# Hand-made semaphore waits, and quarter-row tiles over the end of a row-maximum kernel

## The chip, the cores and the metric

The kernel runs on one core of one Trainium2 chip. The metric is the device time of one execution in microseconds (us). "Before" measured 1261.12 us as the median of three runs (1261.06 to 1261.18).

## The reference

```python
# x: (32, 2048, 2048) float32, about one element in ten is NaN; axis = -1
def reference(x, axis):
    return np.nanmax(x, axis=axis).astype(np.float32)
```

The input is 536.87 MB and the output is 65,536 numbers, so the kernel is a stream: nearly all of its time is the loading of the input.

## The kernel before

The 65,536 rows stand on 128 partitions, 512 rows of 2048 elements on each. A tile is seven rows a partition (the very first has one). Every tile is described by three lists: its loads, its pieces and its row maxima. Each piece runs through three engines:

1. ScalarE makes a 16-bit key from the upper half of each element, in which a NaN stands for the smallest number.
2. GpSimd, or ScalarE itself where the count is negative (a "back-copy"), writes the cleaned upper halves back into the tile.
3. VectorE takes row maxima of the tile as ordinary floats.

There are three buffers for tiles and three for keys, and a key buffer holds three rows. A load may start when the last maximum of the tile that had its buffer is done.

```python
TILES = (
    [([1], [1], [1])]
    + [ ([7], [2, 3, 2], [2, 3, 2]), ([7], [2, 3, 2], [2, 3, 2]), ([7], [2, 3, -2], [2, 3, 2]) ] * 19
    # ... [cut: fifteen tiles whose loads and pieces get smaller] ...
    + [([1, 1, 1, 1, 1, 1, 1], [1, 1, 1, -1, 1, 1, -1], [1, 1, 2, 1, 1, 1])]
)
GROUPS = [TILES[:14]] + [TILES[i : i + 12] for i in range(14, 74, 12)]
# ... [cut] ...
        for loads, pieces, reds in g:
            xt = io.tile([P, WIDE * D], i32, tag="xt")          # one of 3
            at = 0
            for c in loads:
                nc.sync.dma_start(out=xt[:, at * D : (at + c) * D], in_=xg[...])
                at += c
            # ... [cut]
            for c in pieces:
                back, c = c < 0, abs(c)
                xp = xt[:, at * D : (at + c) * D]
                if used + c > KEYS:                             # a new key buffer
                    kt = mid.tile([P, KEYS * D], u16, tag="kt") # one of 3
                    used = 0
                # ... [cut: ScalarE key, then ScalarE or GpSimd back into xt]
                while reds and done + reds[0] <= at:
                    n = reds.pop(0)
                    nc.vector.tensor_reduce(out=acc[...], in_=xt[...], op=ALU.max)
        # after each group: two small VectorE instructions on its maxima
        # ("the flags", for rows without any number); all stores at the very end
```

A scheduler derives the waits between these instructions from the buffers, and it may also reorder the instructions of one engine.

## Time and profile before

| | before |
|---|---|
| device time, median | 1261.12 us |
| span of the profiled run | 1259.46 us |
| first input packet starts | 1.75 us |
| last input packet ends (called **E** below) | 1245.97 us |
| VectorE's last instruction ends | 1256.50 us, E + 10.53 |
| from there to the span's end | 2.96 us |

How to read it: the time is the start, the transfer, and what follows the last packet. The transfer takes 99% and cannot be shortened by reordering work, so the argument is about a dozen microseconds at the end. The prediction shows the lines for this. It also uses the costs of one row by shape, from the groups split by shape (line, engine, operation and tiles, count; then busy us and mean ns of one; then idle time before them):

```profile
L153 DVE TENSOR_REDUCE acc<-xt 128x1 f32<-128x2048 f32 x20 | 44.6, 2276 | 9.2 <-POOL xt L142 9.2
L125 ACT ACTIVATE kt<-xt,top 128x2048 uint16<-128x2048 int16 x45 | 87.3, 1990 | 6.6 <-DMA xt<-in_x_dram 6.5
L142 POOL TENSOR_SCALAR xt<-kt 128x2048 int16<-128x2048 uint16 x34 | 84.3, 2481 | 14.1 <-ACT kt L125 11.9
L134 ACT ACTIVATE xt<-kt 128x2048 int16<-128x2048 uint16 x11 | 27.4, 2488 | 0.3
```

One row thus costs 1.99 us for a key, 2.48 us for the cleaning on either engine, and 2.28 us for the maximum. One after the other that is 6.75 us.

### The profile page before, as it was taken

What the parts mean: (1) busy time and instruction counts of PE and PEld (TensorE: products, weight loads), DVE (VectorE), ACT (ScalarE), POOL (GpSimd) and SP (SyncE); (2) the same over time, 40 slices, a digit from 0 to 9 for tenths busy, and PEclk for the clock granted to TensorE, in tenths of its full rate; (3) what the DMA queues carried; (4) which work ended last, traced back from release to release, by engine and by line L of the source; (5) the groups of instructions that cost most, each with busy time, mean ns of one, the idle gap of its engine ahead of it and who ended that gap; (6) DMA issues with size and microseconds to landing.
All of it is one profiled execution on the core that took longest, in us unless ns stands there. A gap on an engine that the chain in (4) does not pass through costs nothing.

```text
span 1259.5 us, 1258 instructions
## 1 busy us (share of the span) xinstructions
DVE 1115.2 (89%) x242; ACT 1053.3 (84%) x281; POOL 1091.2 (87%) x219
## 2 busy tenths in 40 slices
DVE  0888898888899898888989888999888889999999
ACT  4788797887888878878888788797887899799997
POOL 2989989889898898898988989889889896999996
DMA  9999999999999999999999999999999999999995
GB/s 412 437 437 437 437 424 421 437 438 437 435 433 435 417 435 437 437 435 435 435 426 424 437 437 434 435 435 436 419 433 437 433 438 435 420 432 429 427 425 214
DMA packets 14697, 537.21 MB, mean 427 GB/s; under 512 B 2400, under 2 KB 2400, under 8 KB 2400
## 3 DMA queue, kind: packets, MB, share of 16 engines
q1 hardware_dynamic: 14688, 537.14, 98.9%
q14 instruction: 9, 0.07, 0.0%
HBM read 536.87 MB, written 0.26 MB: 426 GB/s over the span
## 4 chain that ended last, share of the span: by engine, by line
DMA 29%; POOL 27%; ACT 20%; issue 17%; DVE 7%; SPq 0%; ACTq 0%; POOLq 0%; DVEq 0%
DMA xt<-in_x_dram 29%; POOL xt L142 27%; ACT kt L125 16%; DVE acc L153 7%; ACT xt L134 4%; SPq L110 0%; DVE none L164 0%; DVE acc L173 0%; ACTq L125 0%; POOLq L142 0%; DVEq L153 0%; ACTq L134 0%
## 5 line engine op out<-in xcount | busy, mean ns | idle before, releaser
L153 DVE TENSOR_REDUCE acc<-xt 128x2 f32<-128x4096 f32 (+2 forms) x229 | 1112.6, 4916 | 140.0 <-POOL xt L142 140.0
L142 POOL TENSOR_SCALAR xt<-kt 128x4096 int16<-128x4096 uint16 (+2 forms) x215 | 1091.0, 5074 | 159.1 <-ACT kt L125 146.7
L125 ACT ACTIVATE kt<-xt,top 128x4096 uint16<-128x4096 int16 (+2 forms) x247 | 927.9, 3821 | 196.7 <-DMA xt<-in_x_dram 196.5
L134 ACT ACTIVATE xt<-kt 128x4096 int16<-128x4096 uint16 (+1 forms) x32 | 127.5, 3983 | 1.0
L94 ACT ACT_TABLE_LOAD x1 | 1.3, 1283 | 0.7 <-PEq L193 0.7
L164 DVE TENSOR_SCALAR none<-acc 128x84 int32<-128x84 f32 (+1 forms) x6 | 1.5, 251 | 0.2
L173 DVE TENSOR_TENSOR acc<-acc,none 128x84 int32<-128x84 int32 (+1 forms) x6 | 1.5, 243 | 0.2
L92 DVE MEMSET top<- 128x1 f32 x1 | 0.1, 59 | 0.8 <-PEq L193 0.8
L193 POOL MEMSET const-float32-0.0<- 128x1 f32 x1 | 0.1, 99 | 0.2 <-issue 0.2
L94 ACT ACTIVATE warm<-top 128x1 f32<-128x1 f32 x1 | 0.2, 203 | 0.0
L193 POOL MEMSET const-uint8-127<- 128x1 uint8 x1 | 0.1, 103 | 0.0
L193 POOL MEMSET const-bfloat16-1.0<- 128x1 bf16 x1 | 0.1, 102 | 0.0
L193 POOL MEMSET const-float32-1.0<- 128x1 f32 x1 | 0.1, 99 | 0.0
## 6 DMA issues: line engine op xcount, KB each, us to landing
xt<-in_x_dram SPq DMA_DIRECT2D x63, 7168.0 KB, 23.5
xt<-in_x_dram SPq DMA_DIRECT2D x10, 2048.0 KB, 25.3
xt<-in_x_dram SPq DMA_DIRECT2D x5, 3072.0 KB, 16.1
xt<-in_x_dram SPq DMA_DIRECT2D x13, 1024.0 KB, 23.2
xt<-in_x_dram SPq DMA_DIRECT2D x3, 4096.0 KB, 25.1
xt<-in_x_dram SPq DMA_DIRECT2D x1, 6144.0 KB, 23.3
xt<-in_x_dram SPq DMA_DIRECT2D x1, 5120.0 KB, 18.5
out_dram<-acc SPq DMA_DIRECT2D x5, 42.0 KB, 10.7
```

The lines of the kernel that those rows point to most:

```text
L92: nc.vector.memset(top, EDGE)
L94: nc.scalar.activation(out=warm, in_=top, func=ACT.Prelu, alpha=0.5)
L125: nc.scalar.activation(out=kp, in_=xp.bitcast(i16)[:, 1::2], func=ACT.Prelu, bias=top, scale=-1.0, alpha=float(TOP - LOW) / (EDGE - NAN),)
L134: nc.scalar.activation(out=xp.bitcast(i16)[:, 1::2], in_=kp, func=ACT.Copy, bias=float(TOP), scale=-1.0,)
L142: nc.gpsimd.tensor_scalar(out=xp.bitcast(i16)[:, 1::2], in0=kp, scalar1=-1.0, scalar2=float(TOP), op0=ALU.mult, op1=ALU.add,)
L153: nc.vector.tensor_reduce(out=acc[:, base + done : base + done + n], in_=xt[:, done * D : (done + n) * D] .bitcast(f32) .rearrange("p (c d ...
L164: nc.vector.tensor_scalar(out=none, in0=acc, scalar1=NONE, scalar2=float(0x00C00000), op0=ALU.is_equal, op1=ALU.mult,)
L173: nc.vector.tensor_tensor(out=bits, in0=bits, in1=none, op=ALU.bitwise_or)
L193: nc = _bacc.Bacc("TRN2", target_bir_lowering=False, num_devices=1)
```

## The change

The scheduler's waits are replaced by hand-made ones: a class notes for every instruction which semaphore values it needs, drops those already implied, and puts the last one on the instruction itself. And counts become quarter rows, so that the last eighteen tiles (56 to 73 in the diff) can be cut finer. The last group, twelve tiles before, becomes ten and two, so that the last store has 14 columns, not 84. The maxima stay whole rows everywhere: all their counts are multiples of four. There are 112 loads for 96, 255 pieces for 247 and 226 maxima for 229.

```diff
+Q = D // 4
-    + [([7], [2, 3, 2], [2, 3, 2])] * 2
-    + [([1, 6], [-1, 3, 1, -2], [4, 3])]
... [cut]
-    + [([1, 1, 1, 1, 1, 1, 1], [1, 1, 1, -1, 1, 1, -1], [1, 1, 2, 1, 1, 1])]
+    + [([28], [12, -8, 8], [20, 8])]
+    + [([28], [11, 12, -5], [8, 20])] * 3
... [cut]
+    + [([4, 3, 2, 3, 4, 3, 1, 1, 1, 1, 2, 2, 1], [4, -2, 1, 2, 3, 4, 3, -2, 1, 2, 3, -1], [4, 4, 4, 4, 4, 4, 4])]
-GROUPS = [TILES[:14]] + [TILES[i : i + 12] for i in range(14, 74, 12)]
+GROUPS = [TILES[:14]] + [TILES[i : i + 12] for i in range(14, 62, 12)] + [TILES[62:72], TILES[72:]]
+LANES = 14
+class Order:
... [cut]
+    def add(self, who, engine, issue, deps, lane=None, step=1):
+        want = self.needed(who, deps)
+        for s, v in want[:-1]:
+            engine.wait_ge(self.sems[s], v)
+        inst = issue()
+        for s, v in want[-1:]:
+            inst._wait_ge(self.sems[s], v)
+        name = lane or who
+        inst.then_inc(self.sem(name), step)
... [cut: loads take turns at 14 semaphores, "lanes"; a load waits for the last load of its lane]
+                    if used + c > KEYS:
+                        key = (key + 1) % NKEYS
+                        used = 0
+                        kold, kfree[key] = kfree[key], []
+                        if at + c == sum(loads) * Q:
+
+                            kold = kold + kfree[(key + 1) % NKEYS]
... [cut: the same operations as before, each through add()]
```

When the last piece of a tile opens a new key buffer, its ScalarE instruction waits for that buffer but also for the users of the next one.

## The prediction

> **What bounds the kernel now.** I read the page first (shares, slices, queues), then the groups split by shape, the waits of the engines and of the loading queue, and last the timeline and narrow windows over the end.
>
> ```profile
> span 1259.5 us, 1258 instructions
> DVE 1115.2 (89%) x242; ACT 1053.3 (84%) x281; POOL 1091.2 (87%) x219
> ...
> GB/s 412 437 437 437 437 424 421 437 438 437 435 433 435 417 435 437 437 435 435 435 426 424 437 437 434 435 435 436 419 433 437 433 438 435 420 432 429 427 425 214
> ...
> q1 hardware_dynamic: 14688, 537.14, 98.9%
> q14 instruction: 9, 0.07, 0.0%
> ```
>
> The input is 536.87 MB and the load queue is busy 98.9% of the span. The dips in the GB/s row are packets that straddle a slice's edge: in the packet records loads follow each other without a hole from 1.75 us to the end. So the body is transfer time, and 1259.5 us can shrink only at the two ends.
>
> ```profile
> SPq L110 <- DVE acc L153: 1072.0, 66, 27.0
> SPq L110 <- DVE none L164: 84.6, 5, 17.1
> SPq L110 <- DMA xt<-in_x_dram: 27.7, 8, 9.6
> ```
>
> This is the loading queue's own list. It waits nearly always for the row maxima to free a buffer; the scheduler's waits for an older load cost 27.7 us of the queue's time, but only late in the run. By the records even the tightest load there is issued over 3 us before its first packet starts, and the one-row loads of the last tile some 17 us before. None of these waits empties the transfer engines.
>
> ```profile
> 1095.28 28.30 DVE L153 TENSOR_REDUCE acc<-xt 128x3 f32<-128x6144 f32 x8 [1.60 <-POOL xt L142]
> 1124.93 56.28 DVE L153 TENSOR_REDUCE acc<-xt 128x3 f32<-128x6144 f32 x12 [1.35 <-POOL xt L142]
> 1182.00 73.94 DVE L153 TENSOR_REDUCE acc<-xt 128x4 f32<-128x8192 f32 x22 [0.79 <-POOL xt L142]
> 1255.97 0.25 DVE L164 TENSOR_SCALAR none<-acc 128x84 int32<-128x84 f32 x1
> 1256.26 0.24 DVE L173 TENSOR_TENSOR acc<-acc,none 128x84 int32<-128x84 int32 x1
> ...
> 1243.00:1244.00 1.00, 1.00 (x1) 1.00 (x2) 0.00 (x0) 1.00 0.91 254
> 1244.00:1245.00 1.00, 1.00 (x2) 1.00 (x1) 0.00 (x0) 1.00 0.24 82
> 1245.00:1246.00 1.00, 1.00 (x2) 1.00 (x2) 0.47 (x1) 1.00 0.13 41
> ```
>
> Two things set the end. VectorE runs its last 22 maxima (34 rows, 73.94 us) without a gap, so it is behind when data stops. And data stops raggedly: most transfer engines are done by 1243.4, the slowest at 1245.97 (the DMA share falls 0.91, 0.24, 0.13). From that last packet to the end of the last VectorE instruction (1256.50) are **10.53 us**; store and closing barriers take 2.96 more, and the measured time is 1.66 above the span.
>
> **What the Trainium skill says.** "DMA: Bandwidth & Descriptors", section "Where 436 GB/s comes from", gives a port ceiling of 435 GB/s; the 437 of the full slices agrees, so the body is at the limit. "ScalarE: Activation LUTs", section "What ACT_TABLE_LOAD costs", gives 280 ns + 0.833 ns per element for an ACTIVATE with a pointer bias, and about 93 ns of overlap back to back. The trace agrees: 1990, 3698 and 5402 ns at 2048, 4096 and 6144 elements. "VectorE: DVE Perf Modes", section "The DRAIN you can't avoid", says a semaphore after each operation cost nothing extra in its test; here separate wait records take about 0.02 us and stand beside running work. "Runtime: NRT & Kernel Launch", section "Instruction fetch mechanics", says a sequencer fetches its program by DMA as it runs, sequentially, in 16 KiB blocks. The trace has nine such packets during the run, of 8192 bytes each; each holds one of the 16 transfer engines for about 0.31 us.
>
> **The change, part by part.**
>
> *Waits.* The builds hold 390 separate wait or semaphore instructions before on the four engines (110 ScalarE, 100 VectorE, 99 GpSimd, 81 Sync) and 55 after. At 0.02 us that is under 7 us over four engines, beside work and under the transfer time: worth 0 in the body. Indirectly, the instructions of the four fall from 1259 to 970, so perhaps five fetches instead of nine. The slowest transfer engine is about 2.6 us behind the fastest at the end, of which some 0.35 is there from the first load; if the rest follows the fetches, four fewer give 4/9 of 2.3, about 1.0. I take **-0.8 us** on the last landing.
>
> *Loads.* 112 instead of 96. In the packet records 8192 bytes take 0.312 us and 57,344 take 2.121, so 27.2 bytes per ns and 10.5 ns a packet. An engine moves 8 packets a load: 16 x 8 x 10.5 ns = **+1.35 us**.
>
> *The hand-made section.* Its builds show one more branch and one hop over Sync's semaphore before the first load, and after the last store another hop, a drain on each engine, three semaphore steps and a branch. Closing steps in this trace stand 0.06 to 0.09 us apart: **+0.15 us** at the head, **+0.45 us** at the tail.
>
> *Quarter rows.* The maxima stay whole rows (all counts are multiples of four quarters), so VectorE's work is unchanged, 226 maxima for 229. What shrinks is what lies ahead of them. From the groups by shape, for one, two, three and four quarters: ScalarE key 0.71, 1.14, 1.57, 1.99 us; ScalarE back-copy (2488 and 4766 ns) 0.78 and 1.35 for one and two; GpSimd (2481 and 4772 ns) 0.77, 1.34, 1.91, 2.48; VectorE 2.28 a row, the next starting 2.19 after.
>
> I step through the last tile by hand, with E the last packet and 0.45 us to ScalarE (an estimate from the 0.48 to 0.54 us idles there). Counting the last loads back from E: the ninth lands at E-3.96, the eleventh at E-1.98, the twelfth at E-0.69.
> - Pieces six to eight keep ScalarE busy from E-7.47 to E-2.95, the eighth's back-copy to E-1.57.
> - Piece nine (one quarter) ends at E-0.98, piece ten (two) at E+0.07; GpSimd cleans ten by E+1.49, and row six is whole.
> - Piece eleven (three quarters) waits for ScalarE, not for data: E-0.02 to E+1.55; GpSimd to E+3.54.
> - Piece twelve (one quarter): E+1.46 to E+2.17, back-copy to E+2.98.
> - VectorE: row six E+1.53 to E+3.81, row seven E+3.72 to E+6.00; the two flag instructions end at **E+6.56**.
>
> Against 10.53 before this saves 3.97 us, if VectorE reaches the last tile without arrears. It gets the chance: in the old timeline its gaps from 1020 us on add to 10.4 us, each for a first piece not yet clean, and the new tiles there begin with smaller pieces. The same hand chain with the old one-row pieces gives about E+7.85, so VectorE's arrears were 2.7 us of the 10.53.
>
> *Sum.* Last landing 1245.97 + 1.35 + 0.15 - 0.8 = 1246.67; VectorE's end 1253.23; with 2.96 + 0.45 the span is 1256.64; with 1.66 the time is **1258.3 us**, 2.8 less than now.
>
> **The rivals.**
> - *Arrears stay.* If VectorE is still 2.7 us behind, the end is about 1261.0. For: it runs at 2.19 us a row against 2.42 that a row takes to arrive (16.94 us by the records for seven), so it catches up only 0.23 a row. Against: the 10.4 us of gaps. Perhaps one in five, mostly in part.
> - *The loading queue starves.* Three new tiles end with a five-row maximum, 10.8 us (an estimate from the row of shapes, 2.14 a row and 0.14) where two rows took 4.41, so their buffers come free up to 6.4 us later. Loads lead by some 3 to 5 us there; the tiles' shorter last pieces give part of it back, and I reckon 0.5 to 1.3 us of lead left. A hole would add itself to the end, at most about 1 us a tile, and less where the slowest transfer engine still has work. It would make 1259 to 1261.
> - *Waits were the cost.* If the removed waits bound the body, the time would fall by more than 5 us. The 98.9% and the gapless loads speak against it: transfers alone reach to about 1244, and a whole row's maximum and the store must follow. More than 2% (25 us) would need transfers above the port ceiling.
> - *Small loads are dearer.* Packets of 2048 bytes are not in the old trace; were they twice as dear as the line gives, the five one-quarter loads would cost 3 us more. Unlikely, since 8192 bytes lie on the line.
>
> **Range and chances.** 1258.3 in the middle; fewer fetches or a cheaper section give 1256.3 at best, arrears or a starved tile 1260.8. Nothing here approaches 25 us: same 0.98, faster 0.01, slower 0.01.
>
> **What would show it.** Right: VectorE's last instruction ends 6 to 7.5 us after the last packet (10.53 now), its last idle lies after 1235 us rather than at 1182, no hole between loads, fewer instruction packets on q14, about 3.4 us from there to the span's end. Wrong: a gapless VectorE from before 1200 to the end (arrears), a falling DMA share near 1000 to 1040 us (starving), or a first packet well after 1.9 us (the section's entry). A DMA share far below 1 in the body, or a gain above 6 us, would overturn the whole reading.

## The result

| | before | after |
|---|---|---|
| device time, median of 4 runs | 1261.09 us (1260.92 to 1261.18) | 1258.3 us (1257.99 to 1258.64) |
| ratio, 95% interval | | 0.9978 (0.9961 to 0.9995) |
| span of the profiled run | 1259.46 us | 1256.86 us |
| first input packet | 1.75 us | 1.97 us |
| last input packet, E | 1245.97 us | 1247.23 us |
| VectorE's end | E + 10.53 | E + 6.76 |
| from there to the span's end | 2.96 us | 2.87 us |

The change gains 2.8 us or 0.2%. The span's 2.60 us are 1.26 us lost at E, 3.77 gained after it and 0.09 gained in the tail.

The page of the kernel after, in the lines that answer to those shown of before (busy time, GB/s in 40 slices, and the queues with packets, MB and share of 16 engines):

```profile
span 1256.9 us, 966 instructions
DVE 1115.5 (89%) x241; ACT 1058.2 (84%) x292; POOL 1093.9 (87%) x224
...
GB/s 413 438 436 429 420 438 438 438 433 429 423 438 438 436 436 433 418 438 438 436 436 433 420 436 438 438 436 431 418 438 436 434 409 432 432 430 428 426 422 277
...
q1 hardware_dynamic: 17136, 537.14, 99.3%
q14 instruction: 8, 0.07, 0.0%
```

VectorE works as long as before, and the counted instructions fall from 1258 to 966 without a change in the GB/s of the full slices. The loading queue stays as it was: its own list of waits (us in total, times, longest) has the maxima as the reason, and the scheduler's waits for older loads are no longer there.

```profile
SPq L206 <- DVE acc L174: 1068.7, 65, 36.8
SPq L206 <- DVE none L174: 84.9, 5, 17.3
```

The end of the timeline (start, length, engine, line and operation, how many, idle time before and what ended it), and two narrow windows (length, then busy shares of VectorE, ScalarE and GpSimd with instructions, then clock, DMA share and GB/s):

```profile
1222.45 22.08 DVE L174 TENSOR_REDUCE acc<-xt 128x1 f32<-128x2048 f32 x10
1244.71 8.86 DVE L174 TENSOR_REDUCE acc<-xt 128x1 f32<-128x2048 f32 x4 [0.17 <-POOL xt L170]
1253.82 0.17 DVE L174 TENSOR_TENSOR acc<-acc,none 128x14 int32<-128x14 int32 x1
...
1246.00:1247.00 1.00, 1.00 (x2) 1.00 (x3) 0.92 (x2) 1.00 0.93 234
1247.00:1248.00 1.00, 1.00 (x1) 1.00 (x2) 0.81 (x2) 1.00 0.22 46
```

VectorE now waits for data once more, at 1244.71, where before it had run without a gap since 1182.00. After that last wait it has four rows left. At 1245.97 the old kernel's data was complete; here input packets still keep about 3 of the 16 transfer engines busy between 1246 and 1247 us, so the end is won although data arrives later. The DMA share of 0.93 in that window is not the input: by the packet sizes about four fifths of it are the stores of the earlier groups, which were issued behind the loads and start only as engines finish theirs. Of the 0.91 between 1243 and 1244 us, which the prediction reads as the end of the data, about two thirds are stores too.

One thing in the engines' waits I had not predicted. It is ScalarE's list after:

```profile
ACT kt L166 <- DMA xt<-in_x_dram: 141.3, 52, 15.0
ACT kt L166 <- POOL xt L170: 48.3, 37, 2.6
```

Before, ScalarE waited for loads only, 196.5 us in 49 times. Now it waits for GpSimd 37 times, 48.3 us in all. This is the early key wait.

### The profile page after: what moved, and what is told of

Same layout as the page of the kernel before. It is cut to its first block, busy times and chain, and to the rows that moved or that the text cites. A ratio compares the mean times of both kernels' runs of the same rounds, so it can differ in the third digit from the quotient of the medians. Undisturbed runs are those within 1.5% of the kernel's fastest.

```text
span 1256.9 us, 966 instructions
## 1 busy us (share of the span) xinstructions
DVE 1115.5 (89%) x241; ACT 1058.2 (84%) x292; POOL 1093.9 (87%) x224
## 4 chain that ended last, share of the span: by engine, by line
POOL 51%; ACT 29%; DVE 10%; DMA 8%; issue 1%; SPq 1%; ACTq 0%; DVEq 0%
POOL xt L170 51%; ACT kt L166 22%; DVE acc L174 10%; DMA xt<-in_x_dram 8%; ACT xt L166 7%; SPq L206 1%; DVE none L174 0%; ACTq L105 0%; SPq L355 0%; DVEq L105 0%; SPq L105 0%; SPq L162 0%
## 5 line engine op out<-in xcount | busy, mean ns | idle before, releaser
L174 DVE TENSOR_REDUCE acc<-xt 128x2 f32<-128x4096 f32 (+3 forms) x226 | 1112.7, 4980 | 137.0 <-POOL xt L170 136.8
L170 POOL TENSOR_SCALAR xt<-kt 128x4096 int16<-128x4096 uint16 (+9 forms) x220 | 1093.7, 4971 | 156.9 <-ACT kt L166 143.8
L166 ACT ACTIVATE kt<-xt,top 128x4096 uint16<-128x4096 int16 (+10 forms) x255 | 934.7, 3712 | 190.3 <-DMA xt<-in_x_dram 141.3
L166 ACT ACTIVATE xt<-kt 128x4096 int16<-128x4096 uint16 (+6 forms) x35 | 125.8, 3596 | 1.1
```

What stands on the lines that cost most here:

```text
L166: return order.add("act", nc.scalar, lambda: nc.scalar.activation(**kw), deps)
L170: "pool", nc.gpsimd, lambda: nc.gpsimd.tensor_scalar(**kw), deps
L174: return order.add("dve", nc.vector, lambda: do(**kw), deps)
```

## The experiments

**My theory** after the result: the waits themselves are worth nothing, and the gain comes from the new tiles: VectorE's arrears taken away in the middle ones, and a shorter last chain in tile 73. **The rivals:** the hand-made waits bring the gain; the loading queue is starved near 1020 us and some gain is lost there; the last store or the number of load semaphores matters. The first four kernels below ran together, beside before at 1261.28 us; the other eight ran later in two sets of four, with a median of 1261.34 us for before in either. Each time is the median of five runs. All results were correct.

### Hand-made waits with the old tiles

```diff
-TILES = ( ... quarter-row tiles ... )
+TILES = [tuple([n * 4 for n in counts] for counts in tile) for tile in ROW_TILES]   # tiles of before
-GROUPS = ... [TILES[62:72], TILES[72:]]
+GROUPS = [TILES[:14]] + [TILES[i : i + 12] for i in range(14, 74, 12)]
```

> The hand-made order of waits with the old tiles (every count times four) and the old groups. Theory A (the gain is the finer work at the end; waits are worth nothing in the body, and only shorten the last landing by fewer instruction packets): VectorE is as much in arrears as before, so 1260.6 us, at most 0.8 below the old kernel, with 6 to 8 instruction packets on q14 instead of 9 and the slowest transfer engine some 1.8 us behind the fastest instead of 2.6. Theory B (the waits gave the gain): 1258.3 us, as the whole change.

Measured: 1268.93 us (1268.84 to 1269.05), ratio 1.0061 (1.0048 to 1.0073). This is 7.65 us *slower* than before, and neither theory had it. ScalarE's waits and the timeline show where it goes:

```profile
ACT kt L166 <- POOL xt L170: 69.0, 39, 5.5
...
1084.27 15.21 DVE L174 TENSOR_REDUCE acc<-xt 128x3 f32<-128x6144 f32 x3 [3.09 <-POOL xt L170]
1089.09 14.51 ACT L166 ACTIVATE kt<-xt,top 128x6144 uint16<-128x6144 int16 x4 [4.79 <-POOL xt L170]
1101.68 28.31 DVE L174 TENSOR_REDUCE acc<-xt 128x3 f32<-128x6144 f32 x8 [2.20 <-POOL xt L170]
1109.06 14.88 ACT L166 ACTIVATE kt<-xt,top 128x4096 uint16<-128x4096 int16 x6 [5.46 <-POOL xt L170]
```

The early key wait stops ScalarE for 4.79 and 5.46 us, VectorE goes without work for 3.09 and 2.20 us, its buffers come free late, and the loads run dry: the GB/s row of this run falls to 397 and 413 in two of the slices from 1077 us, where before has 420 and 432. E moves from 1245.97 to 1249.90 us. So I had overlooked a part of the change: a wait *added*.

### The new tiles under the old scheduler

```diff
 # before.py, with Q = D // 4 and every count in quarters:
-TILES = ( ... ); GROUPS = ... range(14, 74, 12)
+TILES = ( ... of after ... ); GROUPS = ... [TILES[62:72], TILES[72:]]
```

> The new tiles and groups under the old scheduler's waits. Theory A: 1258.5 to 1259.2 us, nearly the whole gain; some 0.2 us earlier first load, but nine or more instruction packets and a slowest transfer engine 2.6 us behind. Theory B: 1261 us or more. A third possibility: the scheduler's eight load semaphores hold back the one-quarter loads, and the transfer engines run empty in the last tile; then over 1260 and a DMA share well below 1 before 1244 us.

Measured: 1259.20 us (1259.08 to 1259.40), ratio 0.9984 (0.9971 to 0.9996). The tiles alone give 2.1 of the 2.8 us. The rest is seen in the timelines round tile 56, first of this kernel, then of the change:

```profile
968.44 4.74 ACT L144 ACTIVATE xt<-kt 128x4096 int16<-128x4096 uint16 x1
973.27 19.47 DVE L163 TENSOR_REDUCE acc<-xt 128x5 f32<-128x10240 f32 x3 [6.94 <-issue]
```

```profile
964.54 4.76 ACT L166 ACTIVATE xt<-kt 128x4096 int16<-128x4096 uint16 x1
969.44 19.53 DVE L174 TENSOR_REDUCE acc<-xt 128x5 f32<-128x10240 f32 x3 [1.17 <-POOL xt L170]
```

The scheduler puts ScalarE's third key ahead of the second piece's back-copy, so the back-copy starts at 968.44 and not at 964.54 us, and the five-row maximum that needs it starts 3.8 us later. The tile's buffer comes free at 988.4 instead of 984.6, the next load is issued at 988.48, and the packet records show overlong packets there and a hole: for 0.19 us no engine has an input packet, and from 987.4 us until the new load starts each engine stands idle for 1.7 us on average. The hand-made waits keep the order of the program. That, rather than any cheaper wait, is what I find the hand-made part to be worth here; it fits the difference of about 0.9 us between the medians (of different rounds) and of 0.65 us between the two Es (1247.88 and 1247.23), but I did not test it by giving the scheduler the other order.

### Only the last tile new

```diff
 # tiles of before, but
+TILES[73] = ([4,3,2,3,4,3,1,1,1,1,2,2,1], [4,-2,1,2,3,4,3,-2,1,2,3,-1], [4]*7)
```

> Hand-made waits, the new last tile, the old tiles before it. If VectorE's arrears set the old end (theory A), the finer last tile alone is worth little: about 1260.4 us, VectorE without a gap from about 1182 us on. If the last tile's own chain from landing to maximum set it (theory C), most of the gain shows: about 1258.5.

Measured: 1269.19 us (1268.99 to 1269.31), ratio 1.0062. The early key wait hid whatever this was to show; its repeat without that wait stands below.

### Only the middle tiles new

```diff
-TILES[73] = ([4,3,2,3,4,3,1,1,1,1,2,2,1], [4,-2,1,2,3,4,3,-2,1,2,3,-1], [4]*7)
+TILES[73] = ([4]*7, [4,4,4,-4,4,4,-4], [4,4,8,4,4,4])      # the old one-row tile
```

> Hand-made waits, the new tiles before the last, the old one-row last tile. Theory A (both ends are needed: arrears worked off, and a short last chain): about 1260.2 us, VectorE with an idle gap after 1230 us because it has caught up, last instruction 8 to 9 us after the last packet. If arrears alone were the cause: about 1258.5.

Measured: 1261.07 us (1260.89 to 1261.67), ratio 0.9999 (0.9985 to 1.0012). VectorE has caught up, and it does not help:

```profile
1244.66 5.76 ACT L168 ACTIVATE kt<-xt,top 128x2048 uint16<-128x2048 int16 x3
1244.82 6.70 DVE L176 TENSOR_REDUCE acc<-xt 128x2 f32<-128x4096 f32 x2 [2.17 <-ACT xt L168]
1250.45 2.48 ACT L168 ACTIVATE xt<-kt 128x2048 int16<-128x2048 uint16 x1
1251.78 4.48 DVE L176 TENSOR_REDUCE acc<-xt 128x1 f32<-128x2048 f32 x2 [0.27 <-POOL xt L172]
1256.51 0.17 DVE L176 TENSOR_TENSOR acc<-acc,none 128x14 int32<-128x14 int32 x1
```

It idles 2.17 us before the last rows and ends at E + 9.54 all the same (E is 1247.13 here). The one-row keys queue at ScalarE: three run back to back from 1244.66, and only then follows the last row's back-copy. So without arrears the old last tile still takes 9.54 us after the last packet, of the 10.53 before. The early key wait plays no part in this: from 1180 us on ScalarE waits for loads alone here. Theory A fits in kind, with 9.54 us for the 8 to 9 expected and a time 0.9 us above its figure.

### No early key wait, old tiles

```diff
-                        if at + c == sum(loads) * Q:
-
-                            kold = kold + kfree[(key + 1) % NKEYS]
```

> The hand-made waits with the old tiles, without the three lines that let the last key piece of a tile also wait for the next key buffer (each buffer is still waited for by its own next user). The first waits-only kernel took 1268.9 us, and ScalarE waited 69.0 us for GpSimd there, which the old kernel never does. If that early wait is the cause (theory D), the ScalarE waits for GpSimd fall to near 0 and the time to 1260.6, within 0.6. If the hand-made waits are slow in another way, it stays above 1265.

Measured: 1261.52 us (1261.41 to 1261.77), ratio 1.0002 (0.9989 to 1.0014).

```profile
ACT kt L166 <- DMA xt<-in_x_dram: 196.6, 48, 14.9
...
1182.29 73.95 DVE L174 TENSOR_REDUCE acc<-xt 128x4 f32<-128x8192 f32 x22 [0.76 <-POOL xt L170]
```

ScalarE no longer waits for GpSimd at all, and the 7.4 us are back. VectorE's last stretch is the one of before, 73.95 us for 22 maxima, 0.3 us later. The time is 0.3 us above the range that was expected, and not below before: removing the scheduler's waits is worth nothing, within 0.14% either way. E came 0.24 us earlier here (1245.73) and that did not help, because VectorE is in arrears.

### No early key wait, with the change's tiles

The same three lines are taken out of the kernel after.

> The changed kernel without the early wait for the next key buffer. Theory D: ScalarE's 48.3 us of waits for GpSimd go, the loads of the body are issued about 1 us earlier ahead of their first packets (2.2 to 2.7 us now, 3.6 to 3.9 in the old kernel), and the long first packets from 885 to 1000 us go. The end gains little, since the tiles at the end were cut for that wait: 1257.6 to 1258.4 us. If the early wait earns something by saving wait instructions, the time would rise.

Measured: 1258.48 us (1257.97 to 1258.52), ratio 0.9976 (0.9962 to 0.999). The early key wait costs nothing that can be told with the new tiles, and it earns nothing, though it saves instructions: without it the trace has 1032 and with it 966. From 1040 us on ScalarE waits for GpSimd for about 1.0 us in all, against 15.1 us with the old tiles (and without the early wait it waits 1.0 us there for itself): the new pieces seldom open a key buffer where the next one is still in use. As expected, the overlong packets from 885 to 1000 us are gone; those from 1004 us on stay. The time is just above the range expected.

### No early key wait, only the last tile new

The same three lines are taken out of the kernel of "only the last tile new".

> As the earlier kernel with only the last tile new (1269.2 us), but without the early wait, which had spoilt it. Theory A (VectorE's arrears set the old end): 1260.3 us within 0.5, VectorE without a gap from about 1182 us on. Theory C (the last tile's own chain did): 1258.5.

Measured: 1262.10 us (1261.98 to 1262.22), ratio 1.0006 (0.9994 to 1.0019). I had expected a gain from this, and there is none: the time is 1.8 us above theory A's figure and 3.6 above theory C's, which is refuted.

```profile
1182.64 43.36 DVE L181 TENSOR_REDUCE acc<-xt 128x4 f32<-128x8192 f32 x10 [0.76 <-POOL xt L177]
1226.45 30.73 DVE L181 TENSOR_REDUCE acc<-xt 128x1 f32<-128x2048 f32 x13
1257.42 0.17 DVE L181 TENSOR_TENSOR acc<-acc,none 128x14 int32<-128x14 int32 x1
```

VectorE runs without a wait for data from 1182.64 to the end. Pieces that are clean earlier are of no use to an engine that is behind. It even ends 0.8 us later than in the run without this tile: it starts 0.35 us later, the flags of the shorter group stand for 0.45 us in between, and one maximum more is made up for by smaller flags at the end.

### The load near 1020 us, re-cut

```diff
+for i in (56, 57, 58, 59):
+    TILES[i] = ([28], [8, 12, -5, 3], [8, 12, 8])
```

> The changed kernel with tiles 56 to 59 given a first piece of eight quarters and maxima of 8, 12 and 8 instead of first pieces of 11 or 12 and a five-row maximum. In the changed kernel's trace the loads from 886 us on, and most at 1021.5 us, are issued only 1.6 to 2.7 us before their first packet, and those first packets take 0.2 to 1.8 us longer than usual. If that is the loading queue being late, the long first packets vanish, the last packet comes 0.6 to 1.1 us earlier, and the time falls to 1257.3 to 1257.9 us. If the long packets come from elsewhere, they stay and the time stays at 1258.3.

Measured: 1258.13 us (1257.92 to 1258.34), ratio 0.9974 (0.9961 to 0.9986). In the change, load 61 is issued at 1019.55 us, its first packets start 1.6 us after its issue ends, and they take 1.47 to 3.65 us where packets of their size take 1.364. The excess is 9.3 us over 16 engines, and there is no hole to be seen. With these four tiles the long packets at 1020 us are gone and E comes at 1246.92 instead of 1247.23. E gains 0.3 us where 0.6 to 1.1 were expected, and the time, above its range, cannot be told from the change's own.

### Both mended

The re-cut tiles 56 to 59, and no early key wait.

> Both mended: no early wait, and tiles 56 to 59 with a first piece of eight quarters. All long first packets should go (excess of packet time apart from the start and the instruction packets near 0, now 9.3 us over 16 engines at 1020 us alone), the last packet come by 1246.6 us, and the time be 1257.4 to 1258.1 us, the best of all. If it is 1258.3 or more, the late loads never cost anything at the end.

Measured: 1258.15 us (1257.95 to 1258.22), ratio 0.9975 (0.9962 to 0.9987). From 885 us on the only packets overlong by more than 0.05 us are four beside an instruction packet (by 0.35 to 0.66 us) and one at 1055.73 (by 0.2). E is 1246.90, not the 1246.6 expected, and VectorE ends at 1253.59, 0.4 us before the change, but the times overlap: the change has 1257.99 to 1258.64 in other rounds. It separates neither from the change nor from the run with the re-cut tiles alone (1258.13).

### Fewer load semaphores

```diff
-LANES = 14
+LANES = 8
```

> Eight load semaphores instead of fourteen, as the scheduler had. The trace of the changed kernel has the loading queue stuck up to 7 us on single issues late in the run, with about ten loads in flight, so more semaphores than ten should buy nothing, and eight still leave over 5 us of loads ahead: 1258.3 us, within 0.3. If fourteen were needed: over 1259.

Measured: 1258.81 us (1258.57 to 1258.95), ratio 0.9979 (0.9966 to 0.9993). In the change, with about ten loads in flight, the loading queue sticks up to 7.0 us on one issue (at 1200.02 us). With eight semaphores it waits on those instead and no issue takes over 1 us. Loads stay at least 10 us ahead in that stretch of the change, and VectorE ends at E + 6.64: neither form of waiting is on the path. The time is 0.2 us above the range expected. The 0.5 us between the medians I leave open; the intervals against before overlap widely.

### Quarter-row maxima in the last tile

```diff
+TILES[73] = (TILES[73][0], TILES[73][1], [4, 4, 4, 4, 4, 4, 3, 1])
```

> The last row's maximum in two steps of three and one quarters, which the code of the change allows and its tiles do not use. Were the end the chain behind the last landing, 1.4 us would go: 1256.9. If VectorE's own list is the bound in the last four rows, as its 0.2 us of slack before the last maximum says, the split only adds a fixed cost: 1258.3 to 1258.5.

Measured: 1259.16 us (1258.10 to 1259.43, the widest spread of all these runs), ratio 0.998 (0.9968 to 0.9993).

```profile
1250.97 1.74 DVE L176 TENSOR_REDUCE xt<-xt 128x1 f32<-128x1536 f32 x1
1252.75 0.69 DVE L176 TENSOR_REDUCE acc<-xt 128x1 f32<-128x513 f32 x1
```

The split last row takes 1.74 + 0.69 us, a whole one 2.28, and it starts no earlier than VectorE is free. In the change GpSimd's last cleaning ends at 1251.05 and row seven's maximum starts at 1251.30: it waits for VectorE itself by about 0.25 us, so no more than that can be won here. The median is above the range expected, but the profiled run took 1258.49 us and VectorE ends at E + 6.79: what made the slowest runs is not seen.

### The old groups

```diff
-GROUPS = ... + [TILES[62:72], TILES[72:]]
+GROUPS = [TILES[:14]] + [TILES[i : i + 12] for i in range(14, 74, 12)]
```

> The changed kernel with the last twelve tiles in one group again, so that the last flag pair and the last store take 84 columns instead of 14. By the two traces the flag pair costs 0.14 us more and the store 0.18 more: 1258.6 us. If the groups were worth more, 1259 or over.

Measured: 1258.54 us (1258.38 to 1259.09), ratio 0.9978 (0.9966 to 0.9991). From the start of its issue to its landing the last store of 84 columns takes 1.52 us here and 1.66 before; one of 14 columns takes 1.48 in the change and 1.82 with the new tiles under the old scheduler. So its size does not show, and the tail is 2.92 for 2.87 us. The difference is too small to be found in the time.

### Taken together

| waits | old tiles | new tiles | only 73 new | only 56 to 72 new |
|---|---|---|---|---|
| the scheduler's | 1261.3 | 1259.20 | | |
| hand-made, without the early key wait | 1261.52 | 1258.48 | 1262.10 | |
| hand-made, with it | 1268.93 | 1258.3 | 1269.19 | 1261.07 |

## Why the prediction was right, and where its steps were not

The number was right to the tenth, and that is luck: several of its terms were not right, and they cancelled. Even the step from the span to the time is one of them: it is 1.78 us run by run, not 1.66, and the profiled run of the change is the slowest of its four (1258.64 for the median of 1258.3).

- **What bounds the kernel** held: the body is transfer, only the ends move, and the waits bound nothing. The third rival, that the removed waits were the cost, falls with 1261.52 us for waits without the early key wait.
- **"Worth 0 in the body"** for the waits was right for the waits removed and blind to one added. I counted wait instructions (390 and 55) and did not read the condition under which one was put in. With the old tiles that one condition costs 7.4 us (1268.93 against 1261.52). The prediction survived because the new tiles meet it rarely.
- **The last landing** was predicted at 1246.67 and came at 1247.23. The head was +0.22 for 0.15. For the loads I use the run without disturbance, "both mended". The first transfer engine is out of loads when the first of the waiting stores starts: at 1242.95 us before, 1243.32 with the old tiles and no early key wait, and 1244.45 here. Against before that is 1.50 us, 0.21 of it the head; against the other, which has the same head, 1.13. So 16 loads cost 1.1 to 1.3 us where I had 1.35: this term held. Packets of 2048 bytes took 85 to 87 ns against 86 from the line, so the rival of dearer small packets is refuted.
- **The step with the fetches failed.** "Four fewer give 4/9 of 2.3": before the last input packet there were seven against nine, so two fewer (the eighth on the page comes at 1256.73 us). The lag was misread too: from the first engine out of loads (1242.95) to the slowest (1245.97) it is 3.02 us before, not 2.6. In the change it is 1.76, but not through fetches alone: late loads held up the fast engines, and the first engine is out of loads 2.52 us later than before, about 1 us more than head and loads explain. Over the runs the lag does not follow the fetches: ten went with 1.01 us (the run with the hole), eight with 2.05 to 2.47, seven with 1.46 to 2.41. The runs whose loads were not late have 3.02 with nine and 2.41 to 2.46 with eight, which goes the predicted way, but one fetch between kernels that differ in more does not show it. In "both mended" head and loads leave -0.4 to -0.6 us of E for all else, where I had -0.8 for the fetches. What sets the lag stays open.
- **The chain after E** was E + 6.56 by hand and E + 6.76 by measurement, 6.69 with both mended. The pieces cost what the line between shapes gave (0.70 us measured for 0.71 for a one-quarter key, 0.765 for 0.77 for its cleaning, 0.778 for 0.78 for a back-copy). What was mis-sized is where the chain starts: piece six, which I had at E-7.47, begins at E-7.12, when its load has landed (E-7.20), and from there ScalarE stays 0.3 us late. GpSimd has row six clean at E+1.80 for E+1.49, and row seven's maximum ends at E+6.34 for E+6.00. The two flag instructions on 14 columns then take 0.42 us for the 0.56 that I had from 84 columns.
- **Its split between arrears and pieces failed.** "VectorE's arrears were 2.7 us of the 10.53" rested on E + 7.85 for one-row pieces without arrears. The run with only the middle tiles new measured E + 9.54, because the keys queue at ScalarE. So taking the arrears away alone brings 0.99 us there, less than the later landing costs, and the finer last tile then brings 2.78 (9.54 to 6.76). The finer last tile without the middle tiles brings nothing. Both limits stand at the end, and the later one decides; the sum in the prediction came out right because it stepped through both at once.
- **The first rival, arrears that stay,** did not come: VectorE waits for row four until 1244.71. But the margin is thin. It idles 0.17 us there, and rows five to seven are clean only 0.25, 0.08 and 0.25 us before it takes them. VectorE's idle gaps from 1020 us on shrank from 10.4 to 4.9 us, so its own list and the last tile's chain now end almost together, and neither alone has much left to give.
- **The second rival, starving,** happened in a form that I had not thought of: no hole, but packets up to 2.3 us longer where a load was issued only 1.6 us ahead. It moved E by about 0.3 us. The four tiles' pieces of 11 and 12 quarters at their start, which make the first maximum late, belong to it as well as the five-row maxima; the run that mended them changed both at once, so they are not told apart.
- **The tail** was predicted at 3.41 and measured 2.87. The 0.45 us for the section's exit do not show: from the landed store to the end it is 1.36 us for 1.27 before, and the store took 1.48 us for 1.66; both vary by more than this between the other traces.

In sum: E was 0.56 too early and the chain 0.20 too short, the tail 0.54 too long, so the span was missed by 0.22 us.

## What to carry to other kernels

In a stream whose body is at the transfer limit, step through the last tile by hand from the last packet, and ask of each engine both when its data is ready and when it is free: shortening one of the two alone brought nothing here, both together 2.8 us. When waits are replaced, read the new conditions as closely as the old ones, for with the old tiles one added wait cost more than 300 removed ones could give. And a sum that comes out right is no proof of its terms: only the runs that undid one part each showed which of them were.

## What the Trainium skill lacked or had wrong

- "Runtime: NRT & Kernel Launch", section "Instruction fetch mechanics", has blocks of 16 KiB. The instruction queue's packets in these traces are of 8192 bytes and come one at a time (before at 229.1, 258.7, 282.0 and 648.6 us and so on), half such a block each; that a block is fetched in two packets is not seen here.
- "DMA: Bandwidth & Descriptors", section "Latency and other measured facts", does not have what a late load costs while other transfers still run: issued 1.6 us ahead, its first packets took 1.47 to 3.65 us instead of 1.364, without a hole between packets.
- No page that I read says that the issuing queue itself can stick with many loads in flight: with about ten, one issue took up to 7.0 us, and with at most eight none took over 0.5 us.
